# Recasting the SSD stage of a two-layer decoder step as a pinned four-part sequence of pairs

## The chip, the core and the metric

The kernel runs on one core of a Trainium2 chip. The metric is the device time of one launch in microseconds (us); the kernel before takes 2357.1 us (median of three runs, 2356.55 to 2357.26). Profiles hold one execution; its engines are PE (TensorE, matmuls and transposes), DVE (VectorE), ACT (ScalarE), POOL (GpSimd) and SP (SyncE, which issues most DMAs).

## The reference

A trunk of two layers is run once for 512 prompt tokens and 64 sample tokens (8 sequences of 8), all as 576 columns. Layer 0 mixes tokens by a Mamba-2 state-space block (SSD), layer 1 by causal pooling; each mixer stands between two half-step SwiGLU blocks, with RMS norms. Only the SSD block matters here:

```python
proj = h @ w_in                                  # 1024 -> z 2048, xBC 4096, dt 32
z, xbc, dt_raw = jnp.split(proj, [D_INNER, D_INNER + CONV_DIM], axis=-1)
xbc, conv_new = causal_dwconv(xbc, conv0, conv_w, conv_b)      # 4 taps, per channel
xbc = jax.nn.silu(xbc)
xs, Bm, Cm = jnp.split(xbc, ...)                 # 32 heads of 64; B, C: 8 groups of 128
dt = jax.nn.softplus(dt_raw + dt_bias);  A = -jnp.exp(a_log)
# ssd_scan, chunks of 128 tokens:
cb = C B^T;  decay = exp(tril(a_cum_l - a_cum_s))
y_diag = (cb * decay) @ (x dt);  chunk_states = B^T (decay_end * x dt)
h_{c+1} = h_c * chunk_decay + chunk_states;  y_off = (C h_c) * exp(a_cum)
y = (y_diag + y_off + d_skip * xs) * silu(z)
y = rmsnorm per group of 256 channels;  return y @ w_out, new states
```

The outputs are the two activations and, for prompt and samples, the new SSM, convolution and pooling states.

## The kernel before

Everything is kept transposed: channels on the 128 partitions, the 576 tokens in the free dimension. float32 matmuls are made of three passes of rounded halves (hi·hi, hi·lo, lo·hi). A **unit** is one 128-column projection of the 1024 model channels: `proj` calls `mm`, and `passes` (L339) issues 2 token halves x 8 channel tiles x 3 = 48 matmuls of 128x288 into one `acc` tile, two PSUM banks of 512 columns. In the SSD stage PSUM holds two `acc` tiles and four one-bank `misc` tiles, handed out in turn; the next user of a bank waits for the readers of the one before. Weights come by DMA into `raw` (`load`, L325), ACT rounds them to `wb` (L317), and POOL takes the rest (L318).

The SSD stage has 32 convolution units (16 of x, 8 of B, 8 of C), 16 gate units z and the output projection (`outproj`). `conv_in` projects, multiplies by the norm (`rb`) into `ext`, copies the saved convolution rows in (`cst`, L636) and the new ones out (`tails`, L641 and L642), and runs the four taps (ACT L645, three on DVE, L647); `silu` finishes them. `crow` (L654) brings in the saved convolution rows by four DMAs through one buffer; PE transposes each (L657). A chain of DVE and ACT instructions makes the step sizes; `spread` (L749) spreads them over partitions.

The work of a head group g (B and C shared by four heads) is `group` (B in token order, C·B products in `cbs`, a block form `bblk`), then two **pairs** of heads (`pair`, j = 0 and 1): transposes of the old state (`nat`, L789) copied to `h0t` (L790), products with C (L795) read by `ch`, transposes of x (L824) read by `xdt`, `xw`, `xs3`, chunk states (L851) summed into `ht` (L857), the masked decays `m` (ACT exps L813, times `cbs` on DVE, L814), the final products (L864, L871, L873) read into `yt` (L875 to L883), and the state update (L840, L843). After a group, `gsum` squares `yt`, `rnat` (L184) sums columns, `rstd` (from L189 on) makes the norm in a row of small DVE operations, `gnorm` applies it.

Order: a scheduler takes the program's instructions and orders each engine's queue by its own estimates of readiness. `keep_in_program_order` (`pin`) holds an instruction behind the pinned instructions ahead of it. In the kernel before, only the last products of a pair are pinned. Once built, each engine's order is fixed, and each engine works its queue in order.

Of the kernel before, what the change touches and what calls it, by code (L numbers as in the profile page):

```python
# [17 lines left out]
P = 128  # L18
# [3 lines left out]
NB = 8  # L22
# [27 lines left out]
def trunk(ctx, tc, x_prompt, x_sample, state_ssm, state_conv, state_pool,  # L50
# [127 lines left out]
    def rnat(accs, width):  # L178
        pt = misc()
        for c, (t0, n) in enumerate(BLOCKS):  # L180
            for h in range(0, P, 64):
                for i, acc in enumerate(accs):
                    t = t0 + h % n
                    PE.matmul(out=pt[h:h + 64, c:c + 1], lhsT=acc[:, t:t + 64], rhs=ones[:, 0:1], start=i == 0, stop=i == len(accs) - 1)  # L184
# [29 lines left out]
    def rbcast(r):  # L214
        pt, pt2 = misc(), misc()
        for c, (t0, n) in enumerate(BLOCKS):
            o = pt[:, t0:t0 + n] if c < 4 else pt2[:, 0:n]
            PE.transpose(out=o, in_=r[0:n, c:c + 1].broadcast_to([n, P]), identity=ident[0:n, 0:n])
# [115 lines left out]
    def passes(pd, w, acts, first, last):  # L334
        for h in range(2):
            n = 0
            for (wh, wl), (ah, al) in zip(w, acts):
                for lt, a in ((wh, ah), (wh, al), (wl, ah)):
                    PE.matmul(out=pd[:, h, 0:HALF], lhsT=lt, rhs=a[:, h * HALF:(h + 1) * HALF],  # L339
                              start=first and n == 0, stop=last and n == 3 * len(acts) - 1)  # L340
                    n += 1

    def mm(pt, w, acts):
        kn = len(acts)
        for k in range(0, kn, 4):
            passes(pt, w[k:k + 4], acts[k:k + 4], k == 0, k + 4 >= kn)
# [240 lines left out]
    def ssd(tail):  # L587
# [5 lines left out]
        with ExitStack() as st:  # L593
# [31 lines left out]

            def proj(c0, w=None):
                pt = acc_tile()
                mm(pt, w or unit(win[:, :, c0:c0 + P], G), hs)
                return pt

            def conv_in(ct):
# [4 lines left out]
                V.tensor_copy(out=es[:, :, 0:3], in_=cst[:, ct].rearrange("p (b e) -> p b e", e=3))  # L636
# [64 lines left out]
            pre = {}  # L701
            for ct in (16, 24):
                pre[ct] = conv_in(ct)
# [41 lines left out]
            V.tensor_scalar(out=mh[0:32], in0=mh[0:32], scalar1=hv[0:32, 2:3], scalar2=None, op0=ALU.mult)  # L745
            def spread():
                pt = misc()
                self_ = sel.rearrange("h a b -> h (a b)")
                PE.matmul(out=pt[:, 0:P], lhsT=self_, rhs=rhs.rearrange("h a b -> h (a b)"), start=True, stop=True)  # L749
# [21 lines left out]
            pin = tc.keep_in_program_order  # L771
# [448 lines left out]
```

## Time and profile before

| | |
|---|---|
| median of 3 runs | 2357.1 us |
| the profiled execution | 2357.4 us, its span 2355.6 us |
| busy share of the span | PE 97%, DVE 80%, ACT 45%, POOL 44% |
| SSD stage | from about 420 to 1000 us of the span |

Busy times are sums of the records of an engine; PE's records overlap, since matmuls are pipelined, so how fast PE goes is read from the start of one to the start of the next. [...] In rows, `out<-in` names tiles, x is a count, and what stands behind the arrow in brackets is what the engine had waited for.

### The profile page before, as it was taken

The numbers are of one execution on the slowest core, as the hardware profiler recorded it, in microseconds if no ns is written. First come the engines' busy times: TensorE is split into PE (matmuls) and PEld (weight loads), VectorE is DVE, ScalarE is ACT, GpSimd is POOL, SyncE is SP. The second block draws the span as 40 slices with busy tenths as digits, with TensorE's granted clock in tenths as the row PEclk, the third lists the DMA queues.
The fourth block names the chain that finished last, engine by engine and source line by source line (L and its number), as shares of the span: only waits on it lengthen the run. The fifth ranks groups of instructions, "written<-read, shape, count | busy, mean of one in ns | idle before, by whom it ended". The sixth has DMA issues, their size and how long they took to land.

```text
span 2355.6 us, 43789 instructions
## 1 busy us (share of the span) xinstructions
PE 2282.7 (97%) x17572; PEld 2241.3 (95%) x17572; DVE 1874.8 (80%) x2950; ACT 1053.1 (45%) x1947; POOL 1030.7 (44%) x796
## 2 busy tenths in 40 slices
PE   8999999999999999989999999999999999999998
PEld 7999999988999999979999999999999899999997
DVE  8987778688887786798877799778876859778876
ACT  6444434455554545354444354334444344344433
POOL 4555440344444444155554535555531325555530
PEclk9999999999999999999999999999999999999999
DMA  5223222243443334412232232323222242322221
GB/s 150 90 90 108 81 90 66 62 138 110 134 135 107 118 110 113 116 57 88 90 108 82 89 99 72 108 64 99 90 81 67 67 117 83 108 68 94 90 73 59
DMA packets 272904, 222.23 MB, mean 94 GB/s; under 512 B 8322, under 2 KB 269042, under 8 KB 272701
## 3 DMA queue, kind: packets, MB, share of 16 engines
q1 hardware_dynamic: 269172, 218.04, 30.4%
q8 instruction: 139, 2.28, 0.4%
q10 hardware_dynamic: 3528, 1.39, 0.2%
q14 instruction: 65, 0.52, 0.1%
HBM read 206.46 MB, written 12.94 MB: 93 GB/s over the span
## 4 chain that ended last, share of the span: by engine, by line
PE 60%; DVE 9%; ACT 1%; DMA 1%; issue 1%; DVEq 0%; SPq 0%; ACTq 0%
PE acc L375 29%; PE acc L339 27%; DVE wh L256 1%; PE acc L554 1%; DVE cacc L647 1%; PE acc L479 1%; DVE ws L1102 1%; DVE m L814 0%; DMA rd<-in_pool_w_out 0%; PE misc L871 0%; DVE wb L318 0%; PE misc L851 0%; PE misc L864 0%; DVE glo L256 0%; ACT m L813 0%
## 5 line engine op out<-in xcount | busy, mean ns | idle before, releaser
L375 PE MATMUL acc<-wh,wb 128*128 128x288 f32 x6888 | 920.4, 295 | 4.2 <-DVE fo L380 2.3
L375 PEld LDWEIGHTS acc<-wh,wb 128*128 128x128 f32 x6888 | 916.1, 189 | 5.9 <-ACT wb L317 3.2
L339 PE MATMUL acc<-ghi,wb 128*128 128x288 f32 x2752 | 550.7, 295 | 0.3 <-DVE x L416 0.3
L339 PEld LDWEIGHTS acc<-ghi,wb 128*128 128x128 f32 x2752 | 441.2, 188 | 0.6 <-DVE x L416 0.5
L317 ACT CAST wb<-raw 128x512 fp32r<-128x512 f32 (+1 forms) x440 | 265.7, 607 | 358.8 <-PE acc L339 151.9
L339 PE MATMUL acc<-glo,wb 128*128 128x288 f32 x1376 | 404.2, 295 | 0.0
L339 PE MATMUL acc<-hhi,wb 128*128 128x288 f32 x1824 | 382.8, 300 | 2.3 <-DVE x L414 0.8
L318 POOL TENSOR_TENSOR wb<-raw,wb 128x512 fp32r<-128x512 f32 (+1 forms) x154 | 211.3, 1374 | 339.5 <-ACT wb L317 330.5
L318 DVE TENSOR_TENSOR wb<-ws,wb 128x512 fp32r<-128x512 f32 x328 | 325.8, 1004 | 15.0 <-ACT wb L317 14.9
L318 DVE TENSOR_TENSOR wb<-raw,wb 128x512 fp32r<-128x512 f32 (+1 forms) x286 | 269.3, 956 | 63.8 <-ACT wb L317 63.3
L317 ACT CAST wb<-ws 128x512 fp32r<-128x512 f32 x328 | 202.5, 621 | 241.0 <-PE acc L375 216.8
L339 PEld LDWEIGHTS acc<-hhi,wb 128*128 128x128 f32 x1824 | 297.8, 190 | 5.7 <-issue 1.6
L416 DVE SCALAR_TENSOR_TENSOR x<-acc,x 128x576 f32<-128x576 f32 x160 | 120.6, 754 | 194.8 <-PE acc L339 194.6
L339 PE MATMUL acc<-hlo,wb 128*128 128x288 f32 x912 | 273.4, 300 | 0.0
L356 POOL TENSOR_TENSOR ws<-raw,ws 128x512 f32<-128x512 f32 x82 | 151.9, 1852 | 246.0 <-DVE wb L318 241.0
L339 PEld LDWEIGHTS acc<-glo,wb 128*128 128x128 f32 x1376 | 257.9, 188 | 0.0
L318 POOL TENSOR_TENSOR wb<-rd,wb 128x512 fp32r<-128x512 f32 x128 | 174.8, 1374 | 184.0 <-ACT wb L317 183.8
L317 ACT CAST wb<-rd 128x512 fp32r<-128x512 f32 x196 | 114.0, 592 | 250.1 <-PE acc L339 219.3
L355 POOL TENSOR_TENSOR ws<-raw 128x512 f32<-128x512 f32 x82 | 124.6, 1520 | 160.4 <-DVE wb L318 160.4
L339 PEld LDWEIGHTS acc<-hlo,wb 128*128 128x128 f32 x912 | 173.0, 190 | 0.8 <-issue 0.2
L353 POOL TENSOR_TENSOR ws<-raw 128x512 f32<-128x512 f32 x82 | 128.4, 1566 | 87.5 <-DMA raw<-in_ffn_w_gate 78.4
L354 POOL TENSOR_TENSOR ws<-ws,raw 128x512 f32<-128x512 f32 x82 | 130.3, 1589 | 7.7 <-DVE wb L318 1.5
(329 smaller groups left out, 2897.5 us busy)
## 6 DMA issues: line engine op xcount, KB each, us to landing
raw<-in_ffn_w_gate SPq DMA_DIRECT2D x41, 1024.0 KB
raw<-in_ffn_w_up SPq DMA_DIRECT2D x41, 1024.0 KB
rd<-in_ffn_w_down SPq DMA_DIRECT2D x80, 512.0 KB
raw<-in_ssd_w_in SPq DMA_DIRECT2D x48, 512.0 KB
m<-ad SPq DMA_DIRECT2D x16, 576.0 KB
nat<-in_state_ssm SPq DMA_DIRECT2D x16, 512.0 KB
out<-nat SPq DMA_DIRECT2D x16, 512.0 KB
raw<-in_ssd_w_out SPq DMA_DIRECT2D x24, 256.0 KB
```

Source lines behind the costliest of these rows:

```text
L256: V.scalar_tensor_tensor(out=o, in0=xs, scalar=g, in1=sub, op0=ALU.mult, op1=ALU.subtract)
L317: S.copy(out=hi, in_=src)
L318: (eng or V).tensor_tensor(out=lo, in0=src, in1=hi.bitcast(F32), op=ALU.subtract)
L339: PE.matmul(out=pd[:, h, 0:HALF], lhsT=lt, rhs=a[:, h * HALF:(h + 1) * HALF], start=first and n == 0, stop=last and n == 3 * len(acts) - 1)
L353: G.tensor_tensor(out=s[0], in0=blk[2], in1=blk[3], op=ALU.add)
L354: G.tensor_tensor(out=s[1], in0=s[0], in1=blk[0], op=ALU.subtract)
L355: G.tensor_tensor(out=s[2], in0=blk[2], in1=blk[0], op=ALU.subtract)
L356: G.tensor_tensor(out=s[3], in0=blk[1], in1=s[1], op=ALU.subtract)
L375: PE.matmul(out=pt[:, m, 0:HALF], lhsT=wb[:, j, k], rhs=hh[k, h][:, slot], start=n == 0, stop=n == 11)
L416: V.scalar_tensor_tensor(out=halves(x[:, d]), in0=pt[:, :, 0:HALF], scalar=scale, in1=halves(x[:, d]), op0=ALU.mult, op1=ALU.add)
L479: PE.matmul(out=pd[:, m, 0:HALF], lhsT=w[:, a, 2 * k + m], rhs=b[:, h * HALF:(h + 1) * HALF], start=n == 0, stop=n == 5)
L554: PE.matmul(out=pt[:, m, 0:HALF], lhsT=wb[:, a, k], rhs=hh[k, b][:, slot], start=q == 0 and k == a == b == 0, stop=q == 1 and k == 3 and a ...
```

## The change

- Every small matmul and transpose of the SSD stage, and the first matmul of each unit, is pinned. PE's order there becomes the order of the program: units stay whole, small ones stand in batches.
- `pair` becomes a generator of four parts: (1) its DMAs; (2) **B**: all transposes of old state and x, with their readers; (3) **C**: products of C with `h0t`, chunk states, state update; (4) **D**: the final products and their readers. Between two batches the loop puts a projection unit: a B or C unit of the next group ahead of part B (U1), the x unit of the next pair ahead of part C (U2), and the gate unit, in even groups with four output units, ahead of part D (U3).
- `taps` is split from `conv_in` and called after the next batch. `ctl` has two buffers. `m` is multiplied by `cbs` in one operation of 128x1152 rather than two. The old-state transposes and part of `group` use an `acc` tile; a pair's two updates take two `misc` tiles at once.
- Small copies go from DVE to ACT: into `ext`, the rest of `tails`, `ht[:, 0]`, `bnat`.
- `conv_state` and part of the last output projection are called elsewhere.

```diff
-    def rnat(accs, width):
+    def rnat(accs, width, held=False):
...
+                    k = PE.matmul(out=pt[h:h + 64, c:c + 1], lhsT=acc[:, t:t + 64], rhs=ones[:, 0:1], start=i == 0, stop=i == len(accs) - 1)
+                    if held:
+                        tc.keep_in_program_order(k)
...
+                    t = PE.matmul(out=pd[:, h, 0:HALF], lhsT=lt, rhs=a[:, h * HALF:(h + 1) * HALF],
+                                  start=first and n == 0, stop=last and n == 3 * len(acts) - 1)
+                    if held and first and h == n == 0:
+                        tc.keep_in_program_order(t)
...
-                mm(pt, w or unit(win[:, :, c0:c0 + P], G), hs)
+                mm(pt, w or unit(win[:, :, c0:c0 + P], G), hs, True)
...
-                V.tensor_copy(out=es[:, :, 0:3], in_=cst[:, ct].rearrange("p (b e) -> p b e", e=3))
+                S.copy(out=es[:, :, 0:3], in_=cst[:, ct].rearrange("p (b e) -> p b e", e=3))
...
-                V.tensor_copy(out=tails[:, ct, 3:27].rearrange("p (b e) -> p b e", e=3), in_=es[:, :, XST - 3:XST])
+                S.copy(out=tails[:, ct, 3:27].rearrange("p (b e) -> p b e", e=3), in_=es[:, :, XST - 3:XST])
...
+                pre[ct] = ext, a
+
+            def taps(ct):
+                ext, a = pre[ct]
+                n = XS0 + NB * XST - 3
                 for k in range(1, 4):
                     V.scalar_tensor_tensor(out=a[:, 0:n], in0=ext[:, k:k + n], scalar=cw[:, k * 32 + ct:k * 32 + ct + 1], in1=a[:, 0:n],
                                            op0=ALU.mult, op1=ALU.add)
-                return a
...
-                    PE.transpose(out=pt[0:96, q * P:(q + 1) * P], in_=s3[:, q].rearrange("p a s -> p (a s)"), identity=ident)
-
-            def pair(g, j, bt, ctl, bnat, bblk, cbs, xst, yt):
+                    pin(PE.transpose(out=pt[0:96, q * P:(q + 1) * P], in_=s3[:, q].rearrange("p a s -> p (a s)"), identity=ident))
...
+            def pair(g, j, bt, ctl, bnat, bblk, xst, yt):
+                yield
+
+                ph, pt, pt2 = acc_tile(), misc(), misc()
+                for b in range(NB):
+                    pin(PE.transpose(out=ph[:, b // 4, b % 4 * P:(b % 4 + 1) * P], in_=nat[:, b], identity=ident))
+                for c, (t0, n) in enumerate(BLOCKS):
+                    o = pt[0:n, c * P:(c + 1) * P] if c < 4 else pt2[0:n, 0:P]
+                    pin(PE.transpose(out=o, in_=xst[:, t0:t0 + n], identity=ident))
+                stack(pt2[:, P:512], xst)
...
+                S.copy(out=h0t[:, 0:4], in_=ph[:, 0].rearrange("p (b n) -> p b n", n=P))
+                V.tensor_copy(out=h0t[:, 4:8], in_=ph[:, 1].rearrange("p (b n) -> p b n", n=P))
+                V.tensor_tensor(out=xw, in0=pt.rearrange("s (c h p) -> s c h p", c=4, h=2), in1=bc(anat[:, 0:4, 2, h0:h0 + 2], 64), op=ALU.mult)
+                V.tensor_tensor(out=xs3, in0=pt2[0:96, P:3 * P].rearrange("s (q h p) -> s q h p", q=2, h=2), in1=bc(wsn[:, :, h0:h0 + 2], 64), op=ALU.mult)
+                S.copy(out=xw3, in_=xs3)
+                V.tensor_tensor(out=xdt, in0=pt.rearrange("s (c h p) -> s c h p", c=4, h=2), in1=bc(anat[:, 0:4, 1, h0:h0 + 2], 64), op=ALU.mult)
+                V.tensor_tensor(out=xds[0:64], in0=pt2[0:64, 0:P].rearrange("s (h p) -> s h p", h=2),
+                                in1=bc(anat[0:64, 4, 1, h0:h0 + 2], 64), op=ALU.mult)
+                V.tensor_tensor(out=xw3[64:96], in0=xs3[64:96], in1=xw3[64:96].bitcast(F32), op=ALU.subtract)
...
+                yield
+
+                pq, stp, pus = misc(), misc(), [misc(), misc()]
+                for b in range(NB):
+                    r = b % 4 * 32
+                    o = SEQ + b // 4 * 32
+                    pin(PE.matmul(out=pq[r:r + 32, (2 + b // 4) * P:(3 + b // 4) * P], lhsT=ctl[:, o:o + 32], rhs=h0t[:, b], start=True, stop=True))
                 for c in range(4):
-                    PE.matmul(out=stp[:, c * P:(c + 1) * P], lhsT=bnat[:, c], rhs=xw[:, c].rearrange("s h p -> s (h p)"), start=True, stop=True)
+                    pin(PE.matmul(out=stp[:, c * P:(c + 1) * P], lhsT=bnat[:, c], rhs=xw[:, c].rearrange("s h p -> s (h p)"), start=True, stop=True))
+                for q in range(2):
+                    pin(PE.matmul(out=pus[q], lhsT=xw3[:, q].rearrange("s h p -> s (h p)"), rhs=bblk[:, q].rearrange("s b n -> s (b n)"), start=True, stop=True))
+
+                ch = wk.tile([P, 2, P], F32, name="ch", bufs=1)
+                V.tensor_copy(out=ch, in_=pq[:, 2 * P:4 * P].rearrange("p (q n) -> p q n", q=2))
                 ht = wk.tile([P, 4, P], F32, name="ht", bufs=1)
-                V.tensor_copy(out=ht[:, 0], in_=stp[:, 0:P])
+                S.copy(out=ht[:, 0], in_=stp[:, 0:P])
                 for c in range(1, 4):
                     for h2 in range(2):
                         s_ = slice(64 * h2, 64 * h2 + 64)
                         V.scalar_tensor_tensor(out=ht[:, c, s_], in0=ht[:, c - 1, s_], scalar=decb[:, c, h0 + h2:h0 + h2 + 1],
                                                in1=stp[:, c * P + 64 * h2:c * P + 64 * h2 + 64], op0=ALU.mult, op1=ALU.add)
+                V.tensor_tensor(out=m, in0=m, in1=cbs.unsqueeze(1).broadcast_to([P, 2, T]), op=ALU.mult)
+                for b in range(NB):
+                    V.scalar_tensor_tensor(out=nat[:, b], in0=nat[:, b], scalar=decp[:, pr, b:b + 1], in1=pus[b // 4][:, b % 4 * P:(b % 4 + 1) * P],
+                                           op0=ALU.mult, op1=ALU.add)
+                nc.sync.dma_start(out=ssm_s[0, :, h0:h0 + 2].rearrange("b h p n -> (h p) b n"), in_=nat)
+                zs = yield
                 pu, py = misc(), misc()
+                for c in range(1, 4):
+                    pin(PE.matmul(out=pu[:, (c - 1) * P:c * P], lhsT=ht[:, c - 1], rhs=ctl[:, c * P:(c + 1) * P], start=True, stop=True))
+                pin(PE.transpose(out=stp[:, 0:P], in_=ht[:, 3], identity=ident))
                 for q in range(2):
+                    pin(PE.transpose(out=pq[:, q * P:(q + 1) * P], in_=ch[:, q], identity=ident))
...
+                pa, pt2 = acc_tile(), misc()
                 for c in range(4):
+                    pin(PE.transpose(out=pa[:, 0, c * P:(c + 1) * P], in_=bt[:, c * P:(c + 1) * P], identity=ident))
+                stack(pt2, bt)
+                for c in range(4):
+                    pin(PE.matmul(out=pa[:, 1, c * P:(c + 1) * P], lhsT=bt[:, c * P:(c + 1) * P], rhs=ctl[:, c * P:(c + 1) * P], start=True, stop=True))
+                pin(PE.matmul(out=pt2[0:64, 2 * P:2 * P + 64], lhsT=bt[:, SEQ:T], rhs=ctl[:, SEQ:T], start=True, stop=True))
+                S.copy(out=bnat, in_=pa[:, 0].rearrange("s (c n) -> s c n", n=P))
+                V.tensor_copy(out=cbs[:, 0:SEQ], in_=pa[:, 1])
...
+            conv_in(0)
+            bc_ = [bt_ctl(0, 0), bt_ctl(0, 1)]
+            taps(0)
+            x_ = xtile(0)
             ys = None
             for g in range(8):
+                bt, ctl = bc_
+                nys = []
+                for j in range(2):
+                    p = 2 * g + j
+                    if g < 7:
+                        conv_in((25 if j else 17) + g)
+                    elif j:
+                        zs = zproj(p)
+                    if j == 0:
+                        if g == 7:
+                            conv_state(2)
+                            conv_state(3)
+                        bnat, bblk = group(bt, ctl)
+                        bc_ = []
                     yt = wk.tile([P, T], F32, name="yt", bufs=3)
+                    work = pair(g, j, bt, ctl, bnat, bblk, x_, yt)
+                    next(work)
+                    if p == 0:
+                        spread()
+                    next(work)
+                    if g < 7 and j == 0:
+                        taps(17 + g)
+                        bc_.append(bt_ctl(g + 1, 0))
+                    elif g < 7:
+                        taps(25 + g)
+                        bc_.append(bt_ctl(g + 1, 1))
+                    if p < 15:
+                        conv_in(p + 1)
+                    else:
+                        outproj(10, 4, range(0, 2))
+                    if g and j == 0:
+                        r = rnat([sqacc], 256, True)
+                    next(work)
+                    if p < 15:
+                        taps(p + 1)
+                        x_ = xtile(p + 1)
                     if g % 2 == 0 and g:
                         outproj(max(2 * g - 6, 0), 4 if g > 2 else 2, range(4 * j, 4 * j + 4))
+                    if p < 15:
+                        zs = zproj(p)
+                    else:
+                        outproj(10, 4, range(2, 4))
+                    work.send(zs)
                     nys.append(yt)
+                    if g and j == 0:
+                        gnorm(g - 1, ys, r)
+                    if p in (8, 14):
                         conv_state(g // 6)
+                ys = nys
                 if g < 7:
+                    gsum(ys)
...
-            outproj(10, 4, range(KD))
+            outproj(10, 4, range(4, KD))
```

PE ahead of the first convolution unit, in the kernel before (`crow` are saved convolution rows, `rr` the norm, `acc2_4805` the unit of B's first group):

```order
L339 MATMUL acc2_4805<-hlo_4593,wb_4178 128x288
L218 MATMUL misc_4635<-ident_78,rr_4622 128x128 x4
L218 MATMUL misc_4636<-ident_78,rr_4622 128x64
L657 MATMUL misc_4680<-ident_78,crow_4678 128x24 x8
L339 MATMUL acc2_4805<-hhi_4592,wb_4178 128x288
```

and changed:

```order
L220 MATMUL misc_4635<-ident_78,rr_4622 128x128 x4
L220 MATMUL misc_4636<-ident_78,rr_4622 128x64
L669 MATMUL misc_4680<-ident_78,crow_4678 128x24 x8
L669 MATMUL misc_4692<-ident_78,crow_4690 128x24 x8
L669 MATMUL misc_4704<-ident_78,crow_4702 128x24 x8
L669 MATMUL misc_4716<-ident_78,crow_4714 128x24 x8
L679 MATMUL misc_4779<-ident_78,vrow_4775 128x3
L343 MATMUL acc2_4805<-hhi_4592,wb_4178 128x288
```

Before, the four sets of `crow` transposes stood between matmuls of three units; now all four stand ahead of the first unit.

PE in the first pair of group 3, in the kernel before (`acc2_7668` is a unit, the `misc` are parts of the pair):

```order
L795 MATMUL misc_7574<-h0t_7561,ctl_7348 32x128 x4
L339 MATMUL acc2_7668<-hlo_4593,wb_7674 128x288
L339 MATMUL acc2_7668<-hhi_4592,wb_7674 128x288 x2
L339 MATMUL acc2_7668<-hlo_4593,wb_7674 128x288
L824 MATMUL misc_7613<-ident_78,xst_7383 128x128 x4
L339 MATMUL acc2_7668<-hhi_4592,wb_7674 128x288
L824 MATMUL misc_7614<-ident_78,xst_7383 64x128
L339 MATMUL acc2_7668<-hhi_4592,wb_7674 128x288
```

and changed, from the end of U2 (`acc2_7565`) through part C to the start of U3 (`acc2_7701`):

```order
L343 MATMUL acc2_7565<-hhi_4592,wb_7571 128x288
L184 MATMUL misc_7632<-ones_83,sqacc_86 64x1 x10
L844 MATMUL misc_7657<-h0t_7529,ctl_7123 32x128 x8
L846 MATMUL misc_7658<-xw_7528,bnat_7472 128x128 x4
L848 MATMUL misc_7659<-bblk_7475,xw3_7531 128x512
L848 MATMUL misc_7660<-bblk_7475,xw3_7531 128x512
L343 MATMUL acc2_7701<-hhi_4592,wb_7704 128x288
```

The small matmuls that were strewn through a unit stand in a batch. The column sums and part C take five `misc` tiles in a row, of four that there are: `misc_7660` takes the bank of `misc_7632`.

DVE at the same place, in the kernel before (`rm` is the first reader of the column sums):

```order
L814 TENSOR_TENSOR m_7930<-m_7930,cbs_7357 128x2x512
L647 SCALAR_TENSOR_TENSOR cacc_7449<-ext_7441,cw_92,cacc_7449 128x600
L637 TENSOR_TENSOR ext_7543<-acc2_7486,rb_87 128x288
L638 TENSOR_TENSOR ext_7543<-acc2_7486,rb_87 128x224
L639 TENSOR_TENSOR ext_7543<-acc2_7486,rb_87 128x8x8
L815 TENSOR_TENSOR m_7585<-m_7585,cbs_7357 64x2x64
L815 TENSOR_TENSOR m_7930<-m_7930,cbs_7357 64x2x64
L189 TENSOR_SCALAR rm_7471<-misc_7460 128x5
L790 COPY h0t_7561<-misc_7568 128x512
```

and changed:

```order
L820 COPY h0t_7529<-acc2_7507 128x512
L827 TENSOR_TENSOR xw3_7531<-xs3_7530,xw3_7531 32x256
L660 SCALAR_TENSOR_TENSOR cacc_7470<-ext_7462,cw_92,cacc_7470 128x600
L935 TENSOR_TENSOR bsp_7474<-bns_7473,bsp_7474 32x256
L859 TENSOR_TENSOR m_7502<-m_7502,cbs_4980 128x1152
L859 TENSOR_TENSOR m_7875<-m_7875,cbs_4980 128x1152
L660 SCALAR_TENSOR_TENSOR cacc_7470<-ext_7462,cw_92,cacc_7470 128x600
L645 TENSOR_TENSOR ext_7622<-acc2_7565,rb_87 128x288
L646 TENSOR_TENSOR ext_7622<-acc2_7565,rb_87 128x224
L647 TENSOR_TENSOR ext_7622<-acc2_7565,rb_87 128x8x8
L191 TENSOR_SCALAR rm_7643<-misc_7632 128x5
```

`rm_7643`, whose end frees the bank for `misc_7660`, stands behind both pairs' multiplications of `m` (`m_7875` is the next pair's) and the reading of U2, as its counterpart did; the `h0t` copy, which stood behind it, stands ahead.

## Rows read from the trace of the kernel before

**Rows 1.** Busy time by window: PE, PEld, DVE, ACT, POOL, granted clock, DMA share, GB/s

```profile
420.00:470.00 50.00, 49.42 (x396) 48.01 (x396) 33.84 (x78) 21.25 (x46) 18.51 (x22) 1.00 0.25 69
470.00:480.00 10.00, 4.69 (x31) 3.90 (x29) 5.83 (x15) 2.35 (x4) 2.67 (x2) 0.85 0.45 128
480.00:1000.00 520.00, 502.93 (x4193) 478.02 (x4193) 416.45 (x928) 264.69 (x567) 213.65 (x200) 0.98 0.41 120
```

**Rows 2.** PE's waits, 423 to 1000 us, the first in total: us, times, longest

```profile
PE misc L795 <- DVE h0t L790: 5.1, 3, 2.5
```

**Rows 3.** Windows again: four at half clock, one of small matmuls, one of units

```profile
477.10:487.30 10.20, 9.13 (x45) 7.87 (x46) 7.14 (x16) 4.14 (x13) 6.37 (x8) 0.50 0.63 186
541.95:545.37 3.42, 3.42 (x17) 3.38 (x16) 3.25 (x12) 1.90 (x4) 0.33 (x1) 0.50 0.00 0
712.60:719.45 6.85, 6.31 (x43) 6.00 (x44) 6.82 (x18) 3.13 (x7) 2.77 (x4) 0.50 0.30 83
941.30:944.70 3.40, 3.40 (x16) 3.35 (x17) 3.16 (x11) 1.27 (x3) 1.27 (x1) 0.50 0.02 5
...
100.00:140.00 40.00, 39.70 (x300) 39.47 (x299) 25.22 (x33) 13.49 (x22) 17.97 (x14) 1.00 0.33 106
...
957.30:963.70 6.40, 5.13 (x46) 3.22 (x44) 6.40 (x14) 4.06 (x7) 1.22 (x1) 1.00 0.46 127
```

**Rows 4.** PE's timeline: a batch, the unit behind it, and the ends of the stretch counted

```profile
480.14 0.47 PE L756 MATMUL misc<-ident,nat 128*128 128x128 f32 x1
...
490.85 0.43 PE L795 MATMUL misc<-h0t,ctl 128*32 128x128 f32 x8
491.21 0.54 PE L339 MATMUL acc<-hhi,wb 128*128 128x288 f32 x2
491.58 0.29 PE L339 MATMUL acc<-hlo,wb 128*128 128x288 f32 x1
...
1000.38 0.47 PE L236 MATMUL misc<-ident,rr 128*128 128x128 f32 x2
```

**Rows 5.** `crow`: its DMA's issues, and PE's waits for it (ns; first to last start)

```profile
L654 SPq DMA_DIRECT2D crow<-in_state_conv x3: 297/321/322, 428.1 to 437.0; - x3
...
L657 PEldq EVENT_SEMAPHORE  x3: 51/51/51, 430.2 to 439.1; - x3
```

**Rows 6.** DVE and ACT by line, 480 to 1000 us: busy us, mean ns

```profile
L647 DVE SCALAR_TENSOR_TENSOR cacc<-ext,cw,cacc 128x600 f32<-128x600 f32 x84 | 86.8, 1033 | 17.9 <-ACT cacc L645 9.4 <-POOL wb L318 7.5
L814 DVE TENSOR_TENSOR m<-m,cbs 128x1024 f32<-128x1024 f32 x16 | 25.3, 1600 | 0.3
L790 DVE COPY h0t<-misc 128x512 f32<-128x512 f32 x16 | 10.9, 679 | 1.1 <-PE misc L789 1.1
L827 DVE TENSOR_TENSOR xw<-misc,anat 128x512 f32<-128x512 f32 x16 | 10.8, 677 | 0.0
L642 DVE COPY tails<-ext 128x24 f32<-128x24 f32 x27 | 10.5, 389 | 0.2
L835 DVE TENSOR_TENSOR xw<-xs,xw 32x256 fp32r<-32x256 f32 x16 | 7.7, 478 | 4.1 <-ACT xw L834 3.8
L832 DVE TENSOR_TENSOR xs<-misc,wsn 96x256 f32<-96x256 f32 x16 | 6.5, 405 | 0.0
L931 DVE TENSOR_TENSOR bsp<-bns,bsp 32x256 fp32r<-32x256 f32 x7 | 5.7, 820 | 0.2
...
L813 ACT ACTIVATE m<-m,anat 128x128 f32<-128x128 f32 (+1 forms) x160 | 48.4, 379 | 1.3 <-DMA dd<-nat 1.2
L790 ACT COPY h0t<-misc 128x512 f32<-128x512 f32 x16 | 9.2, 578 | 2.0 <-PE misc L789 2.0
```

**Rows 7.** DVE's timeline: one reading of a convolution unit

```profile
439.54 0.46 DVE L637 TENSOR_TENSOR ext<-acc,rb 128x288 f32<-128x288 f32 x1
439.91 0.38 DVE L638 TENSOR_TENSOR ext<-acc,rb 128x224 f32<-128x224 f32 x1
440.21 0.21 DVE L639 TENSOR_TENSOR ext<-acc,rb 128x64 f32<-128x64 f32 x1
```

More of the change, by code (lines that the diff above doesn't have):

```diff
@@ L332, in unit, with passes @@
         return [(bl[k // 4][:, 0, k % 4], bl[k // 4][:, 1, k % 4]) for k in range(kn)]
-    def passes(pd, w, acts, first, last):
+    def passes(pd, w, acts, first, last, held=False):
         for h in range(2):
@@ L748, in spread @@
                 self_ = sel.rearrange("h a b -> h (a b)")
-                PE.matmul(out=pt[:, 0:P], lhsT=self_, rhs=rhs.rearrange("h a b -> h (a b)"), start=True, stop=True)
+                pin(PE.matmul(out=pt[:, 0:P], lhsT=self_, rhs=rhs.rearrange("h a b -> h (a b)"), start=True, stop=True))
                 PE.matmul(out=pt[:, P:P + 16], lhsT=self_[0:32], rhs=mh[0:32], start=True, stop=True)
@@ L835, in pair @@
-                V.tensor_tensor(out=xw3[64:96], in0=xs3[64:96], in1=xw3[64:96].bitcast(F32), op=ALU.subtract)
-                def update():
-                    for q in range(2):
-                        pt = misc()
-                        PE.matmul(out=pt, lhsT=xw3[:, q].rearrange("s h p -> s (h p)"), rhs=bblk[:, q].rearrange("s b n -> s (b n)"), start=True, stop=True)
-                        for i in range(4):
-                            b = 4 * q + i
-                            V.scalar_tensor_tensor(out=nat[:, b], in0=nat[:, b], scalar=decp[:, pr, b:b + 1], in1=pt[:, i * P:(i + 1) * P], op0=ALU.mult, op1=ALU.add)
-                    nc.sync.dma_start(out=ssm_s[0, :, h0:h0 + 2].rearrange("b h p n -> (h p) b n"), in_=nat)
@@ L933, in group @@
                     G.tensor_tensor(out=bblk[:, q], in0=bsp[:, q:q + 1].broadcast_to([96, 4, P]), in1=bc(bmask, P), op=ALU.mult)
-                pt = misc()
-                for c in range(4):
-                    PE.matmul(out=pt[:, c * P:(c + 1) * P], lhsT=bt[:, c * P:(c + 1) * P], rhs=ctl[:, c * P:(c + 1) * P], start=True, stop=True)
-                V.tensor_copy(out=cbs[:, 0:SEQ], in_=pt)
-                pt = misc()
-                PE.matmul(out=pt[0:64, 0:64], lhsT=bt[:, SEQ:T], rhs=ctl[:, SEQ:T], start=True, stop=True)
-                S.copy(out=cbs[0:64, SEQ:T], in_=pt[0:64, 0:64])
-                return bnat, bblk, cbs
+                return bnat, bblk
             def gsum(ys, add=True):
@@ L946, in gsum @@
                 S.activation(out=sq, in_=ys[1], func=AF.Square)
-                if not add:
-                    return [sqacc, sq]
-                V.tensor_tensor(out=sqacc, in0=sqacc, in1=sq, op=ALU.add)
-                return rnat([sqacc], 256)
+                if add:
+                    V.tensor_tensor(out=sqacc, in0=sqacc, in1=sq, op=ALU.add)
+                return [sqacc, sq]
             def gtile(g):
@@ L971, in zproj, with bt_ctl, xtile @@
                 return zs
+            cbs = gp.tile([P, T], F32, name="cbs")
+            V.memset(cbs[64:P, SEQ:T], 0.0)
+            def bt_ctl(g, which):
+                if which == 0:
+                    t = gp.tile([P, T], F32, name="bt")
+                    silu(16 + g, t)
+                else:
+                    t = gp.tile([P, T], F32, name="ctl", bufs=2)
+                    silu(24 + g, t)
+                return t
+            def xtile(k):
+                t = wk.tile([P, T], F32, name="xst")
+                silu(k, t)
+                return t
```

131 lines of the change are left out of this document (28 added, 103 removed).

## The prediction

> **What bounds the kernel now.** I read the page first: PE is busy 97% of the span, so that only what PE does not do, or does slowly, can be won. Then the windows, to find the stage that the change touches, and its idle time: 0.58, 5.31 and 17.07 us between 420 and 1000 us [rows 1], 23.0 us together. There the other engines have slack on average (DVE 416 of 520 us, ACT 265), but PE's waits are for DVE: the first in total are for `h0t` copies, 5.1 us in three, the longest 2.5 [rows 2]. Then the granted clock, window by window: it is 0.50 for 10.20, 3.42, 6.85 and 3.40 us, 23.9 us together [rows 3]. At full clock a unit's matmul starts every 0.133 us (300 in 40 us); in the second of these windows 17 take 3.42 us, 0.20 each, so a third of that window is lost; half would be lost if all of it went at half speed. I take 42%, 10.0 us (8 to 12). Last the timeline: behind a batch of small matmuls the first two of a unit take 0.37 us up to the next [rows 4] where 0.27 is the pace. That is 0.10 lost at each return to a unit, and the timeline has 137 batches between its ends in [rows 4].
>
> So PE loses 23.0 idle and 10.0 to the clock, and some 14 to returns: 47 us that a better order could win, in a kernel of 2357.4 us by the profiled execution. The median is 0.3 less, which I neglect.
>
> **The change part by part.** PE's arithmetic is the same, but its order in this stage is now written out; so I take all the old losses off and add up what the new order loses.
>
> *Taken off.* Idle time −23.0, clock −10.0. From the order I count about 50 batches where there were 137: 87 x 0.10 = −8.7 (0 if the loss moves into the batches, −17 if entering a batch costs as much as leaving it). Sum −41.7.
>
> *The start of the stage.* All four sets of `crow` transposes and the one behind them now stand ahead of the first convolution unit, and `crow` has one buffer, so each DMA is issued after the transposes of the one before. From issue to the end of PE's wait it is 430.2 − 428.1 = 2.1 us, and again 439.1 − 437.0 [rows 5]; before, units lay beside it. Three waits of 2.15 with nothing beside them are 6.4 us idle. After the longest idle time of before (5.31 us in 470 to 480) the clock was 0.50 for 10.20 us; the shortest such stretch is 3.40 [rows 1, 3]. At 42% that is 1.4 to 4.3; I take 2.9. Sum +9.3 (7.8 to 10.7). The 5.31 us themselves, a wait for the chain of step sizes, don't come back: that chain starts behind the last of these transposes, whose wait ended at 439.1 us before [rows 5] and some 6 us earlier now, with the units between them gone; DVE has little else to do in the gap, and four units and a `group` still lie ahead of `spread`.
>
> *A first pair (j = 0) of groups 1 to 7.* The second update matmul of part C takes the bank of the column sums, which is free once DVE has run `rm`. PE gets there, counted from the end of part B's transposes of x, after the unit U2, 48 x 0.133 = 6.4, eight small ones in 0.36 [rows 4] and 17 others at 0.133 at most, 2.3: 9.0 us. DVE, which can start part B's readers at the same point, has ahead of `rm`: `xw`, `xdt`, `cbs` and half of `h0t`, 4 x 0.68; `xs3` 0.41; three taps, 3 x 1.03; `xw3` 0.48; `bsp` 0.82; and `m` of this and of the next pair, 2 x 1.60 x 1152/1024 = 3.6 [rows 6]. That is 11.1; neighbours overlap by 0.08 (0.46 long, the next 0.37 later [rows 7]), 12 x 0.08 = 1.0 off; and reading U2, 0.9. DVE is there after 11.1 us, PE after 9.0: PE waits 2.1, and the unit U3 and what follows are queued behind it on PE, and part D's readers on DVE behind those. Seven times: +14.7. The two ends: nothing, if DVE starts earlier than I count or PE's 17 go slower; and half-clock time after each wait, since the one of 2.5 us was followed by 3.40 us at half clock [rows 2, 3], 1.4 each, 9.8 more. I take 2.1 without a clock loss, being nearer to the row's mean wait, 1.7.
>
> *Pairs without a `rnat`* (j = 1): every batch has a unit of 6.4 us ahead of its reader. Part B's readers up to `h0t` take 2.5 us, part C's chain starts with ACT's copy and six short sums; the cover holds, nothing. If it is gone, that is the rival below.
>
> *Five places out of step:* the first pair (its readers meet those of `spread`), two bursts of short output units in group 2, and the last two pairs, where `conv_state` and `group` stand back to back. I take half a wait each, 5 x 1.05 = +5.2 (0 to 10.5).
>
> *Small copies on ACT.* DVE loses 27 copies of 0.39 and as many smaller ones, and one of 0.68 per group; ACT gets them, at 0.58 at most for the largest of them [rows 6]. Both go on beside units; ACT had 255 of 520 us free [rows 1]. Nothing, but if ACT is late its exps are (below). The 128x1152 operation replaces two; its longer part is in the 3.6. The new DMA order moves `m` and the old states one part earlier; they had a unit and more to land and have it still. Nothing.
>
> Sum: 2357.4 − 41.7 + 9.3 + 14.7 + 5.2 = 2344.9, say 2345.
>
> **The rivals.**
>
> *All covered.* DVE no longer does the small copies, and it may begin `m` while PE is still in U1's batch; then the waits of the j = 0 pairs and the five places go, and only the start remains: 2345 − 14.7 − 5.2 = 2325. For it: DVE's 80% in this stage, which falls. Against it: `rm` has 11.1 us of work ahead of it in DVE's queue, and that queue is done in order.
>
> *The next pair's `m` holds up DVE (slower).* The multiplication of the next pair's `m`, ahead of `rm`, waits for ten exps on ACT, 10 x 0.38 = 3.8 us [rows 6], and these for its DMA and POOL's masks. If they start only when the multiplication is due, 3.8 comes to every j = 0 wait, and such a wait of 5.9 us brings half clock, 1.4: 7 x 5.2 = 36.4 more, 2381. It decides from the point where a j = 0 wait costs 2.1 + 12.4/7 = 3.9 us: from there on the change is slower. For it: ACT gets more work, and exps of a later pair ahead of this pair's copies. Against it: ACT is half free, and `m` is fetched a pair ahead.
>
> *Waits only moved.* The j = 0 waits come to just these 3.9 us, from anything that I have not counted on DVE: 2357.
>
> *Batches slow the clock.* In the window from 957.3 us most of PE's work was transposes, with 1.3 us idle, and the clock stayed at 1.00 [rows 3]. Were it not so, each of 16 places where batch B (and at eight of them `group`) stands alone would be followed by 1.4 us lost: 2345 + 22 = 2367. [...]
>
> **How the numbers follow.** The forecast, 2345, gets 0.45; its own range is 2336 to 2354 (returns 0 to 17, waits 1.2 to 3). All covered 0.17, `m` late 0.20, waits moved 0.13, clock 0.05. What a measurement of this kernel can tell from no change is about 0.2%, 4.7 us. Faster: nearly all of the forecast (0.42) and all covered, 0.59 less a little, 0.58. Same: the rest of the forecast, waits moved, and a mild case of `m` late, 0.19. Slower: most of `m` late and the clock, 0.23. The range goes from all covered with the shortest clock loss at the start, 2345 − 19.9 − 1.5 = 2323, to 2345 with the upper ends of the start, of the j = 0 clock loss and a third of the five places (1.4 + 9.8 + 1.8) and with the returns not won (8.7), 2366.
>
> **What would show it.** Right: in the stage's first ten microseconds three idle times of 2 us in front of `crow` transposes; seven waits of 2 us of the second update matmul for DVE `rm`; no wait of 5 us for `rhs`; fewer than 60 batches; the stage some 12 us shorter. Wrong: waits of over 4 us there, or PE waiting for ACT (`h0t`, `ht`); granted clock under 0.98 over the stage; a difference outside the stage.

## The result and the profile after

The changed kernel takes 2386.3 us (median of 4; 2383.1 to 2387.2), the kernel before 2357.2: a ratio of 1.0115 (95% interval 1.0102 to 1.0129). It is slower by 29 us, where I forecast 12 faster; my range ended at 2366.

All of it lies in the SSD stage. From the first transposes of `crow` to the first matmul of the last two output tiles it takes 567.5 us before (427.4 to 994.9) and 597.0 after (426.5 to 1023.5), 29.5 more; the profiled executions differ by 29.8.

The windows of after, in the columns of [rows 1]: the whole stage; a stretch at half clock (granted clock 0.50) at its start; one behind a first pair.

```profile
426.50:1023.50 597.00, 555.21 (x4528) 531.65 (x4527) 413.68 (x896) 294.87 (x703) 227.31 (x222) 0.95 0.39 112
...
429.50:443.20 13.70, 9.10 (x50) 8.90 (x51) 3.82 (x12) 3.33 (x9) 0.00 (x0) 0.50 0.17 49
593.40:600.20 6.80, 5.58 (x23) 5.58 (x24) 6.74 (x10) 1.06 (x3) 2.64 (x2) 0.50 0.26 75
```

PE is idle for 597.0 − 555.2 = 41.8 us, 18.8 more than the 23.0 of [rows 1]. The clock was at half for 54.6 us in nine stretches, where [rows 3] had 23.9. For 10.0 of the 54.6 PE was idle (4.6 and 1.2 in the two stretches shown), and for 1.6 of the 23.9; that is in the idle time already. PE worked at half clock for 44.6 us rather than 22.3, and at the 42% that I had taken, an estimate, 22.3 more cost 9.4. Together 28.2 of the 29.5: the returns to a unit that the change saves (51 batches rather than 143, counted over the whole stage) show no gain. DVE's busy time fell from 452.4 to 413.7 us, and the kernel is slower all the same.

PE's waits in after, 420 to 1035 us (total, times, longest), beside the one row of [rows 2]:

```profile
PE acc L343 <- DVE cbs L931: 17.1, 6, 3.3
PE misc L669 <- DMA crow<-in_state_conv: 7.0, 3, 2.4
PE misc L790 <- ACT s L788: 4.7, 6, 1.0
PE acc L343 <- DVE x L420: 4.3, 2, 3.6
PE misc L848 <- DVE xw L827: 2.2, 2, 1.4
PE misc L869 <- DVE ht L857: 2.0, 4, 0.7
```

The waits for `h0t` are nearly gone and that for `rhs` is gone, as forecast; `crow` is where I put it. The wait for `rm` (L191) that I had priced at 14.7 us isn't there. In its place, in the first pair of groups 1 to 6, U2's *first* matmul waits for the `cbs` copy: six times 2.9 us on average (2.25 to 3.31), and a half-clock stretch of 3.4 or 6.8 us with each, three of which begin in the last 1.3 us of the wait. U2 takes an `acc` tile; of the two, the old-state transposes of part B have just taken one, and the other holds `group`'s products until its readers are done.

Why is that copy late? The timeline of ACT in group 4's first pair:

```profile
725.53 1.28 ACT L837 ACT_TABLE_LOAD   x1 [1.51 <-DMA m<-ad]
726.83 2.92 ACT L837 ACTIVATE m<-m,anat 128x128 f32<-128x128 f32 x10
729.66 0.60 ACT L321 CAST wb<-raw 128x512 fp32r<-128x512 f32 x1
730.16 0.35 ACT L788 COPY s<-xst 128x192 f32<-128x192 f32 x1
...
730.63 0.89 ACT L653 ACTIVATE cacc<-ext,cols,cw 128x600 f32<-128x600 f32 x1
731.42 0.56 ACT L930 COPY bnat<-acc 128x512 f32<-128x512 f32 x1
```

of DVE there:

```profile
727.21 0.22 DVE L647 TENSOR_TENSOR ext<-acc,rb 128x64 f32<-128x64 f32 x1
731.60 0.84 DVE L660 SCALAR_TENSOR_TENSOR cacc<-ext,cw,cacc 128x600 f32<-128x600 f32 x1 [4.17 <-ACT cacc L653]
732.36 0.68 DVE L821 TENSOR_TENSOR xw<-misc,anat 128x512 f32<-128x512 f32 x1
732.96 0.68 DVE L824 TENSOR_TENSOR xdt<-misc,anat 128x512 f32<-128x512 f32 x1
733.56 0.68 DVE L931 COPY cbs<-acc 128x512 f32<-128x512 f32 x1
```

and of PE:

```profile
728.24 1.09 PE L807 MATMUL acc<-ident,nat 128*128 128x128 f32 x8
729.16 0.71 PE L810 MATMUL misc<-ident,xst 128*128 128x128 f32 x5
730.57 0.42 PE L790 MATMUL misc<-ident,s 128*96 128x128 f32 x2 [0.69 <-ACT s L788]
734.29 0.61 PE L343 MATMUL acc<-hhi,wb 128*128 128x288 f32 x1 [3.31 <-DVE cbs L931]
```

The ten exps are those of the *next* pair's `m`. They wait for its DMA, then hold ACT for 4.2 us with the table load. `m` has two buffers, and this DMA is issued as the final products of the pair before this one (L876, L878), which read the same buffer, end; PE and SP have there:

```profile
719.66 0.28 PE L878 MATMUL misc<-m,xd 128*64 128x64 f32 x4
```

```profile
719.98 0.34 SPq L799 DMA_DIRECT2D m<-ad  x1
```

ACT goes on 5.5 us after the issue, having been idle for the last 1.5. Behind the exps stand the s3 copy, the bias step of U1 (L653) and the `bnat` copy. DVE, with nothing wrong of its own, is idle for 4.17 us: the first tap at the head of its queue waits for the bias step. The `cbs` copy comes behind the tap, U2 behind the copy. What ACT lost here to a DMA (1.51 us) and to the exps that came late behind it (4.2) was paid on PE, with 3.31 us in front of U2.

### The profile page after: what moved, and what is told of

It is laid out like the page before. It is cut to its first block, busy times and chain, and to the rows that moved or that the text cites. A ratio compares the mean times of both kernels' runs of the same rounds, so it can differ in the third digit from the quotient of the medians.

```text
span 2385.1 us, 43747 instructions
## 1 busy us (share of the span) xinstructions
PE 2295.6 (96%) x17572; PEld 2257.0 (95%) x17572; DVE 1835.7 (77%) x2847; ACT 1061.4 (45%) x2035; POOL 1025.3 (43%) x796
## 4 chain that ended last, share of the span: by engine, by line
PE 72%; DVE 16%; DMA 4%; ACT 3%; issue 3%; POOL 1%; SPq 0%; ACTq 0%; DVEq 0%; POOLq 0%
PE acc L343 34%; PE acc L381 33%; DVE wb L322 3%; DMA m<-ad 3%; DVE wh L260 1%; DVE cacc L660 1%; ACT m L837 1%; PE acc L485 1%; PE acc L560 1%; DVE nat L861 1%; DVE fo L386 1%; POOL wb L322 1%; DVE ws L1129 1%; DVE fo L389 1%; ACT wb L321 0%
## 5 line engine op out<-in xcount | busy, mean ns | idle before, releaser
L343 PE MATMUL acc<-hhi,wb 128*128 128x288 f32 x1824 | 389.0, 305 | 18.0 <-DVE cbs L931 17.1
L322 DVE TENSOR_TENSOR wb<-ws,wb 128x512 fp32r<-128x512 f32 x328 | 319.7, 986 | 14.6 <-ACT wb L321 14.4
L343 PEld LDWEIGHTS acc<-hhi,wb 128*128 128x128 f32 x1824 | 307.5, 196 | 21.5 <-DVE cbs L931 18.9
L322 POOL TENSOR_TENSOR wb<-raw,wb 128x512 fp32r<-128x512 f32 (+1 forms) x154 | 199.5, 1297 | 291.2 <-ACT wb L321 274.2
L343 PEld LDWEIGHTS acc<-hlo,wb 128*128 128x128 f32 x912 | 178.6, 196 | 0.4
```

The lines of the kernel that those rows point to most:

```text
L322: (eng or V).tensor_tensor(out=lo, in0=src, in1=hi.bitcast(F32), op=ALU.subtract)
L343: t = PE.matmul(out=pd[:, h, 0:HALF], lhsT=lt, rhs=a[:, h * HALF:(h + 1) * HALF], start=first and n == 0, stop=last and n == 3 * len(acts) ...
```

## The experiments

**The exps held behind the bias step (on the changed kernel).** The chain is cut at its first link.

```diff
-                S.activation(out=a[:, 0:n], ..., func=AF.Identity, ...)
+                tc.keep_in_program_order(S.activation(out=a[:, 0:n], ..., func=AF.Identity, ...))
...
-                        S.activation(out=m[0:n, h2, t0:t0 + n], ..., func=AF.Exp, ...)
+                        pin(S.activation(out=m[0:n, h2, t0:t0 + n], ..., func=AF.Exp, ...))
```

> The changed kernel with one thing more: on ACT the exps of m and the bias step of each convolution unit (the write of cacc) are held in the order of the program, so that the next pair's exps can't stand ahead of this pair's convolution unit. Theory A (a chain over three engines: in the first pair of a group the next pair's ten exps wait on ACT for the DMA of m, the bias step waits behind them, DVE's first tap waits for the bias step, the cbs copy waits behind the tap, and U2's first matmul waits for the cbs copy to free one of two acc tiles): PE's 17.1 us of waits for cbs fall below 6, the 54.6 us at half clock in the stage below 35, the time comes to 2352 to 2366. Rival B (two acc tiles are too few wherever the copy stands): waits for cbs stay above 10 us, time above 2375. Rival C (the clock falls because transposes stand in batches, not because PE waits): the waits go, the half-clock time stays above 45 us, time about 2366.

2360.3 us, ratio to before 1.0004 (0.9995 to 1.0014): 26 us won back by an order on ACT alone. The same place, in this run, on ACT and DVE:

```profile
715.77 0.89 ACT L653 ACTIVATE cacc<-ext,cols,cw 128x600 f32<-128x600 f32 x1
...
722.11 1.28 ACT L837 ACT_TABLE_LOAD   x1
```

```profile
716.68 2.09 DVE L660 SCALAR_TENSOR_TENSOR cacc<-ext,cw,cacc 128x600 f32<-128x600 f32 x1 [1.89 <-ACT cacc L653]
718.70 0.68 DVE L931 COPY cbs<-acc 128x512 f32<-128x512 f32 x1
```

and PE's waits:

```profile
PE acc L343 <- DVE cbs L931: 7.2, 5, 2.0
PE misc L669 <- DMA crow<-in_state_conv: 6.7, 3, 2.3
PE acc L343 <- DVE x L420: 5.1, 2, 2.7
```

The bias step now runs before the exps, whose table load comes last. The waits for `cbs` fall to 7.2 us, a little over the 6 that I had expected, and half clock to 34.1 us in the stage (expected: below 35), with the batches as they were. So B is wrong as the main cause. C, the clock falling because transposes stand in batches, isn't it either: with the same 51 batches, most of the half-clock time behind the first pairs went with the waits.

**The cbs copy put ahead of the taps.** The chain is cut at its last link but one, on DVE.

```diff
-                V.tensor_copy(out=cbs[:, 0:SEQ], in_=pa[:, 1])
+                pin(V.tensor_copy(out=cbs[:, 0:SEQ], in_=pa[:, 1]))
...
-                    V.scalar_tensor_tensor(out=a[:, 0:n], ...)
+                    tc.keep_in_program_order(V.scalar_tensor_tensor(out=a[:, 0:n], ...))
```

> The changed kernel with the chain cut at another link: on DVE the cbs copy and the taps are held in the order of the program, which puts the cbs copy of a group ahead of the taps of the unit before it; ACT's order stays. Theory A: waits of U2 for cbs fall below 4 us; waits of the s3 transposes for ACT (4.7 us) stay, and taps come later, so that a part comes back behind column sums or ht; 2356 to 2370. Rival B: waits stay above 10 us, above 2375. Rival C: half-clock time stays above 45 us, about 2368.

2383.0 us, ratio to before 1.0092 (1.0075 to 1.0109): a miss, and not clearly below the changed kernel, whose interval overlaps. The waits for `cbs` are still 11.6 us, and the wait for `rm` that I had priced is there now:

```profile
PE misc L848 <- DVE rm L191: 6.6, 4, 2.8
```

By these numbers it is rival B's outcome. DVE's timeline shows another reason:

```profile
733.52 0.68 DVE L824 TENSOR_TENSOR xdt<-misc,anat 128x512 f32<-128x512 f32 x1
736.03 0.69 DVE L931 COPY cbs<-acc 128x512 f32<-128x512 f32 x1 [1.83 <-ACT bnat L930]
```

The copy waits for ACT itself (1.83 us). `group` now puts the transposes that `bnat` reads and the products that `cbs` reads into one `acc` tile, and the built program makes the second reader wait for the first; the first, moved to ACT by this very change, stands behind the exps.

**The cbs copy cut loose from ACT.** As the last run, with the two copies of `group` swapped, so that `cbs` is the first reader.

```diff
+                pin(V.tensor_copy(out=cbs[:, 0:SEQ], in_=pa[:, 1]))
                 S.copy(out=bnat, in_=pa[:, 0].rearrange("s (c n) -> s c n", n=P))
-                pin(V.tensor_copy(out=cbs[:, 0:SEQ], in_=pa[:, 1]))
```

> The changed kernel with the cbs copy cut loose from ACT: in group, DVE's copy of cbs is written ahead of ACT's copy of bnat, which reads the same acc tile, so that it no longer waits for it; and, as in the run that put the copy ahead of the taps, cbs copy and taps are held in program order on DVE. Theory A2 (the cbs copy was bound to ACT's queue by the shared acc tile, so moving it on DVE alone couldn't help): U2's waits for cbs fall from 11.6 us to under 2; the s3 waits for ACT (6 us) stay, and something of the rest comes back in part C, behind h0t or rm; 2362 to 2374. If the copy's wait for ACT is not what held it: waits for cbs above 8 us, 2378 to 2386.

2391.7 us, ratio 1.0137 (1.0122 to 1.0153): a miss too, and no better than the changed kernel. PE's waits:

```profile
PE acc L343 <- ACT bnat L931: 14.7, 7, 5.3
PE misc L848 <- POOL ext L643: 10.9, 4, 3.1
PE misc L790 <- ACT s L788: 10.5, 7, 2.1
```

The waits for `cbs` are gone, but the tile has a second reader, and U2 now waits for that one, on ACT (14.7 us). The second update matmul (L848), 3.1 us at most, is the place that I had priced in the prediction. The view names a memset of POOL's, which ends by chance at that time; the timeline has `rm` there, on DVE, and PE starting as it ends:

```profile
748.83 0.15 DVE L191 TENSOR_SCALAR rm<-misc 128x5 f32<-128x5 f32 x1
...
749.13 0.62 PE L848 MATMUL misc<-bblk,xw 96*128 96x512 f32 x1 [2.63 <-POOL ext L643]
```

`rm` stands behind the late taps. So DVE's order alone mended nothing: with the exps still ahead on ACT, each link that was cut left another.

**The saved convolution rows in three buffers.** The second and third set go into the two buffers of `m`, which are free then.

```diff
-                crow = dp.tile([27, 2, 512], F32, name="crow")
-                cf = crow[0:24].rearrange("t a b -> t (a b)")
+                if q in (1, 2):
+                    cf = wk.tile([P, 2, T], F32, name="m")[0:24].rearrange("t a b -> t (a b)")[:, 0:1024]
+                else:
+                    cf = dp.tile([27, 2, 512], F32, name="crow")[0:24].rearrange("t a b -> t (a b)")
```

> The changed kernel with the saved convolution rows fetched into three buffers rather than one (the second and third set lie in the two buffers of m, which are free then). Theory A on the start of the stage (PE waits for three DMAs through one buffer, then runs at half clock): the waits for crow fall from 7.0 us to 2 or less, and the 13.7 us at half clock from 429.5 us on shrink or go; 2374 to 2379. Rival C (batches of transposes slow the clock): waits go, half clock of over 10 us stays, 2380. Rival D (the start is hidden, since the chain of step sizes needs its time anyway): a wait of 5 us appears at spread, 2384 to 2388.

2379.7 us, ratio 1.0083 (1.0068 to 1.0098), 6.6 less than the changed kernel. The waits for `crow` are 1.2 us in one rather than 7.0 in three, and the first stretch at half clock is 6.8 us rather than 13.7:

```profile
PE misc L671 <- DMA crow<-in_state_conv: 1.2, 1, 1.2
```

That is as theory A said, at 0.7 us above its range, though a part comes back a little later: a half-clock stretch of 10.2 us from 462.2 where the changed kernel had 6.8 from 470.5.

**All pins taken out of the changed kernel.** `pin` does nothing, and the `held` arguments are left out.

> The changed kernel with all its pins taken out; the program's order of parts and units is kept, the scheduler orders PE freely again. Theory A: the exps of the next pair still stand ahead on ACT, so the waits at the first pairs stay in part; PE may fill some with other work: 2365 to 2390. Rival E (the pinned order on PE is itself what costs): 2360 or less.

2370.7 us (ratio to before 1.0043, 1.0028 to 1.0058): 16 us of the 29 go. With the exps as they are, the order that the scheduler was free to change lost less. This alone doesn't say whether pins cost as such; the last run below does.

**The first two edits that helped, together.**

> The changed kernel with the exps and bias steps held in program order on ACT and the saved convolution rows in three buffers, that is both earlier edits together. Theory A: the two losses add, since they lie in different places: 26 us less than the changed kernel by the one and 6.6 by the other, 2386 to about 2354; waits for cbs about 7 us, for crow under 2. Rival D (the start is hidden by the chain of step sizes): 2360, as with the exps alone, with a wait at spread.

2354.3 us, ratio 0.9980 (0.9972 to 0.9989). The two gains add within 1 us: 2386.3 − 26.0 − 6.6 = 2353.7.

**In group 2, the gate unit ahead of the four short output units,** on top of these two.

```diff
+                    if g == 2:
+                        zs = zproj(p)
                     if g % 2 == 0 and g:
                         outproj(max(2 * g - 6, 0), 4 if g > 2 else 2, range(4 * j, 4 * j + 4))
                     if p < 15:
-                        zs = zproj(p)
+                        zs = zs if g == 2 else zproj(p)
```

> The kernel with exps held and three buffers, and in group 2 the gate unit set ahead of the four short output units. Theory A: the 5.1 us that short output units wait there for additions to x behind taps on DVE go to under 2, and the half-clock time behind them (6.8 us) with them: 5 to 8 us below that kernel, about 2347. Rival F (DVE is full there and the wait moves to part D): 0 to 2 us, waits for ht or yt's readers instead.

2344.4 us, ratio 0.9941 (0.9927 to 0.9954): 10 us less, above the 5 to 8 that I had expected, and faster than both kernels. The window of its stage, and PE's waits in it; that for `x` (L420) is gone:

```profile
424.90:981.70 556.80, 541.13 (x4529) 518.91 (x4528) 411.05 (x896) 297.86 (x704) 227.87 (x222) 0.98 0.42 119
```

```profile
PE acc L343 <- DVE cbs L933: 6.3, 6, 1.8
PE acc L927 <- DVE ext L647: 1.9, 1, 1.9
PE acc L930 <- ACT ctl L916: 1.8, 1, 1.8
```

15.7 us idle and 17.1 at half clock in the stage. That the time is the one that I had forecast for the change is chance: it is another kernel.

**The same, with the cbs copy ahead of the bnat copy.**

> The fastest kernel (2344: exps held, three buffers, gate unit first in group 2) with the cbs copy written ahead of the bnat copy. Theory A2: its 6.3 us of waits for cbs go to under 1.5; 2337 to 2342. If they only move to part C or D: 2343 to 2346.

2347.0 us (0.9946, 0.9933 to 0.9958), no gain. The waits for `cbs` are gone, and what follows them is the wait of the prediction:

```profile
PE misc L850 <- DVE rm L191: 8.1, 6, 2.1
```

Six times 1.35 us, 2.1 at most. With the wait ahead of it taken away, the next in DVE's queue came due.

**The small copies, each way.** In the kernel before, they alone go to ACT; in the kernel with held exps, they alone go back to DVE.

```diff
-                V.tensor_copy(out=es[:, :, 0:3], ...)
+                S.copy(out=es[:, :, 0:3], ...)
...
-                V.tensor_copy(out=tails[:, ct, 3:27]..., ...)
+                S.copy(out=tails[:, ct, 3:27]..., ...)
...
-                V.tensor_copy(out=ht[:, 0], in_=stp[:, 0:P])
+                S.copy(out=ht[:, 0], in_=stp[:, 0:P])
...
-                V.tensor_copy(out=bnat, ...)
+                S.copy(out=bnat, ...)
```

> The kernel before with the small copies alone moved from DVE to ACT. As I priced it, nothing: 2355 to 2360, DVE 25 to 37 us less busy over the stage, PE's waits within 3 us of before. Rival: DVE's slack is what PE waits for, then 5 to 12 us faster; or ACT is late, then slower.

2354.1 us, ratio 0.9984 (0.9975 to 0.9992): about 4 us gained, below what I had called a measurable difference, but with 1 outside the interval. DVE is 23 us less busy over the stage.

> The changed kernel with exps held and the small copies back on DVE. If the copies on ACT are worth something in the new order, it is because DVE's work between part B and the cbs copy or the column sums is on PE's path: 2 to 10 us above 2360 with longer waits for cbs, rm and ht. If they are worth nothing: 2358 to 2362.

2366.9 us, ratio 1.0038 (1.0025 to 1.0051), against 2360.3: the copies on ACT are worth 6.6 us in the new order (8 by the ratios). With them on DVE PE waits longer for `x` (7.0 us rather than 5.1), `ht` (3.8 rather than 1.2), `rr` (3.8) and `rm` (3.0), which the other run does not list; for `cbs`, where I had expected longer waits too, it waits less (4.4 rather than 7.2).

**The control: exps and bias steps held in the kernel before.** The edit is that of the first run.

> A control: the kernel before with exps and bias steps held in program order on ACT, as in the first edit. If holding them is a gain of its own, and not a mending of the new order, this falls by 10 us or more, below 2347. Theory A (the hoisted exps do harm where the next reader is pinned right behind, and before, the free order on PE filled such waits): within 6 us of before, 2351 to 2363.

2353.3 us, ratio 0.9985 (0.9975 to 0.9994): 4 us rather than 26. So holding them mends the new order above all; that the hoisted exps hurt because U2 stands right behind the readers fits this, and the 16 us won back without pins.

**Pins taken out of the fastest kernel.** Only the exps and bias steps on ACT stay held.

> The fastest kernel so far (2344: exps held, three buffers for the saved rows, gate unit first in group 2) with PE's pins taken out. With the changed kernel, taking them out won 16 us. If pins cost as such (rival E), it falls again, to 2340 or less. Theory A: once the readers are on time the pinned order waits little (15.7 us idle in the stage), and the scheduler's own order only brings back waits it doesn't foresee: 2350 to 2365.

2343.9 us against 2344.4: the same. Theory A's 2350 to 2365 is a miss, and rival E's gain doesn't come either. The window of its stage:

```profile
424.90:982.00 557.10, 546.48 (x4497) 518.60 (x4496) 400.21 (x894) 300.94 (x706) 228.33 (x222) 0.99 0.42 118
```

Where the readers were on time, PE's pins were worth nothing in sum, but the two kernels don't lose the same things. Without pins PE is idle for 10.6 us rather than 15.7 and at half clock for 13.7 rather than 17.1; yet the stage is as long, so that, by the same 42%, some 7 us more go while PE works. It has 81 batches rather than 51; whether the 7 us lie at the returns to a unit, no run shows.

## Why the prediction was wrong

The step that failed is "A first pair (j = 0) of groups 1 to 7". I let PE run from part B through U2 "after the unit U2, 48 x 0.133 = 6.4", as if U2 could start at once, and counted one bank, that of the column sums. The diff itself says that `group` and the old-state transposes now take `acc` tiles, of which there are two; U2 is the third in that row. I also let DVE "start part B's readers at the same point", where its queue stood behind a tap that waited for ACT. Measured in place of 14.7 us: 17.1 for `cbs`, 4.7 for the s3 copies, and 30.7 us at half clock at these six places, for 27.3 of which PE worked, at 42% 11.5. That is 33.3, and the difference of 19 is nearly half of my error of 41.

The reason that I gave against a late `m` was that it "is fetched a pair ahead", and under *Small copies* that the loads "had a unit and more to land and have it still". The transfer does land within a unit (5.5 us, a unit is 6.4); what I left out is that its exps stand ahead of this pair's work in ACT's queue, and that so late a landing has them run when the bias step is due.

All parts, in us; those measured are idle times, and 42% of the time that PE worked at half clock:

| | forecast | measured |
|---|---|---|
| old idle time and clock taken off | −33.0 | −32.4 |
| returns to a unit | −8.7 | +1.3, what is left over |
| start of the stage | +9.3 | +10.8 |
| first pairs | +14.7 | +33.3 |
| all other places | +5.2 | +16.5 |
| sum | −12.5 | +29.5 |

The other parts, by the same steps:
- *Taken off.* The old waits did go. The returns to a unit were mis-sized: 8.7 forecast, no gain measured. A step that was 0.10 longer at one return did not sum to 0.10 for each of them.
- *The 42%.* The 0.20 us that I read at half clock is a mean over unit and small matmuls. The unit's alone start 0.24 us apart there, against 0.133 at full clock; so 45% is lost, and the 42%, taken between a third and a half, was near by luck:

```profile
543.62 0.44 PE L339 MATMUL acc<-hlo,wb 128*128 128x288 f32 x1
543.86 0.68 PE L339 MATMUL acc<-hhi,wb 128*128 128x288 f32 x2
544.34 0.44 PE L339 MATMUL acc<-hlo,wb 128*128 128x288 f32 x1
```

- *The start:* 6.4 us idle forecast, 7.0 measured; 2.9 for the clock, where 13.7 us at half clock, of which PE worked 9.1, are 3.8. Three buffers gave 6.6 back. The mechanism was right.
- *Five places out of step:* 5.2 forecast; 4.3 for the short output units in group 2 alone, of which one wait of 3.6 was followed by 3.4 at half clock, and 16.5, with their clock, for all places other than the start and those first pairs. The gate unit set ahead in group 2 gave 10 us.
- *Small copies:* "nothing" was wrong by 4 to 7 us, in the change's favour.
- *The rival that came true* was "the next pair's `m` holds up DVE", at 2381. Its cause was right: exps of the next pair, waiting for their DMA, ahead of this pair's work on ACT. Its place was wrong: not DVE's multiplication of `m` but ACT's bias step, and from there two `acc` readers. I gave it 0.20 because ACT is half free and `m` is fetched early. The free half was no help to what stood behind the waiting exps: in group 4 the bias step's input was there at 727.43 us, and it ran at 730.63.
- *Batches slow the clock* is not the main cause: the fastest kernel has the same 51 batches as the changed one, while half clock in the stage went from 54.6 to 17.1 us. That they slow it, by 1.4 us at each of 16 places, was a rival's supposition. No run shows a batch that brings the clock down alone: in the fastest kernel three of the 51 batches stand beside a half-clock stretch, each with a wait of 1.3 us or more, and in the changed kernel the wait of 3.6 us for `x`, with 24 matmuls of a unit just ahead of it and no batch, was followed by one too. Whether a batch holds back the return of the clock stays open: in the fastest kernel the clock fell at the end of two waits, of 1.9 and 1.8 us, and stayed at half over a batch of 10 us of transposes and small matmuls, with 0.2 us idle, until the unit began:

```profile
460.30:470.50 10.20, 10.02 (x49) 7.95 (x49) 6.72 (x13) 6.55 (x20) 4.18 (x4) 0.50 0.27 71
```

What stays open: why the kernel before gains 4 us from held exps (its profile has 1.9 us less idle time in the stage and 6.8 less at half clock) and as much from the copies (the profiled execution was the slowest of its runs and shows no gain); and how much of the 16 us of the unpinned kernel comes from which of its moves. The wait for the exps' DMA itself wasn't tried: no run fetches `m` earlier.

## What to carry to other kernels

Where an order is written out for one engine, go along the queues of the engines that read for it, and ask of each instruction at the head what it may wait for: exps that came late on ACT, behind a transfer, were paid on PE (17.1 us in front of six units), over a bias step, a tap and a copy, with ACT idle for half of the stage and DVE for three tenths. Count the users of each PSUM pool in the order in which they now come, next to the number of its tiles, and see which engine the last reader of each tile is on. A wait that is worked out for one place may be hidden behind a longer one ahead of it; that for `rm` came back, 8.1 us, when the waits for `cbs` were mended.

## What the hardware showed that I had not expected

A good part of the loss of a wait came as clock: six waits of 2.9 us on average, 17.1 us together, each went with 3.4 or 6.8 us at a granted clock of 0.50, 30.7 us in all, some 11.5 us lost by the estimate above. With the exps held, waits of 2.0 us at most in the same places were followed by one such stretch, of 3.4 us.
